# A hybrid transformer layer on one core: the low parts of the gate and branch weights formed on GpSimd

## The chip, the cores and the metric

The kernel runs on one core of one Trainium2 chip. The metric is the device time of one execution in microseconds (us); several runs are timed and their median is given. A separate execution is recorded by the hardware profiler; its trace gives the rows below.

A core has five engines with a queue each: TensorE (PE, matrix products; PEld is its weight load), VectorE (DVE), ScalarE (ACT), GpSimd (POOL) and SyncE (SP, which here issues nearly all DMAs). An engine takes its instructions in the order written into its queue and waits on semaphores for the others.

## What is computed

One layer of a diffusion backbone over 256 latent and 256 context tokens of width 1024, all in fp32:

```
u   = modulate(rmsnorm(x))                       # latent and context tokens
p   = u @ w_in                                   # ten groups of columns
o_h = HGRN2 linear recurrence(p[0..4])           # 8 heads
o_a = grouped-query attention(p[5..7])           # 8 heads, 2 KV heads
y   = sigmoid(p[8]) * (o_h @ w_branch[0]) + sigmoid(p[9]) * (o_a @ w_branch[1])
x   = x + m * rmsnorm(y @ w_out)
x   = x + m * rmsnorm(moe(modulate(rmsnorm(x)))) # top 4 of 32 experts, w_up 1024x2048, w_down 1024x1024
```

p[8] and p[9] are the gates, w_branch[0] and w_branch[1] the two branches; these are what the change touches.

## The kernel before, in words

The first part (the mixer, up to the router) forms its fp32 products from pairs of reduced-precision products. A weight block is split into a high part (`act.copy` to the type fp32r, L240) and a low part, the difference of the block and its high part (`dve.tensor_sub`, L241), and three matmuls replace one (`mm3`, L246): high by high (L248), high weight by low token (L251), low weight by high token (L252). Only L252 needs the low part of the weights.

Weights come in slabs of 1024 rows by 256 columns (1 MB). `slab` (L225) issues one DMA on SP into a raw tile, of which there are three (tag "raw"), and returns a function that splits half a slab (512 rows: a tile of 128 partitions by 1024 numbers) into a tile of the tag "hl", which holds high and low part and of which there are two. So at most two split halves are alive, and the next ScalarE copy waits until TensorE has used up the half before the last. `chan_major` (L254) uses a half in 24 matmuls of 256 columns.

`branch(br, j)` (L695) makes 256 of the 1024 output columns of one branch: a gate slab (tiles wga, hlga; product pga), its sigmoid, a branch slab (wwb, hlwb; product pb), and the product of both on VectorE (L706 for branch 0; L708, L709, and a split of the sum at L711 and L712 for branch 1). The eight `branch` calls make 16 slabs and 32 halves. The four of branch 0 stand between the attention heads (after heads 1, 3, 5 and 7, L714 to L719), the four of branch 1 follow the last head. `attn_head` (L662) has on VectorE the row maximum (L673), the reciprocal (L677) and the scaling of the softmax (L678, tile pr), whose result TensorE transposes (L681, tile ppt). Between the heads VectorE also sums a product of a modulation vector (L192, tile macc).

After the branches come the output projection (slabs wwo), the second norm, the router, and the experts, whose weights (192 pieces of 2 MB, or parts of one) stream through a ring of ten slots (L897). Some ring slots reuse memory of the mixer: the token tiles "u", free once the last gate is done; the tile "oa" (yg), free after the output projection; and three slots of a pool that opens only after the mixer's slabs are released (L835, L837).

The order of the instructions in the queues of the mixer is not the order of the program text: a planner that walks the program with its own costs for each instruction puts them in order, by priority among those that are ready. Matmuls of different products are mixed by it. In the expert part the order of TensorE is kept as written (L846). A change of an engine or a cost can therefore give other orders on all engines of the mixer.

GpSimd has 16 instructions in the kernel before: constants, two masks, and four DMA issues, two of them for the tile bd (L1081).

Of the kernel before, what the change touches and what calls it, by code (L numbers as in the profile page):

```python
# [39 lines left out]
def hybrid_layer(ctx, tc, x, c, ctx_in, c_ctx, w_mod, b_mod, norm_g, w_in, hgrn_lb, hgrn_norm_g,  # L40
# [3 lines left out]
    pe, act, dve, pool = nc.tensor, nc.scalar, nc.vector, nc.gpsimd  # L44
# [46 lines left out]
    def mmps(name):  # L91
        return ps.tile([P, 512], F32, tag="mm", bufs=4, name=name)
# [7 lines left out]
    def raw_tile(name):  # L100
        return ip.tile([P, 2048], F32, tag="raw", bufs=3, name=name)
# [120 lines left out]
        dve.reciprocal(dst, dst)  # L222


    def slab(src, nm, wr=None):  # L225

        wr = raw_tile("w" + nm) if wr is None else wr
        nc.sync.dma_start(wr.rearrange("p (k f) -> p k f", k=KT), src.rearrange("(k p) f -> p k f", p=P))

        def half(hf):  # L230
            hl = ip.tile([P, 2, 4, 256], F32R, tag="hl", bufs=2, name=f"hl{nm}{hf}")
            hi, lo = hl[:, 0], hl[:, 1]
            split(hi, lo, wr[:, hf * 1024:(hf + 1) * 1024].rearrange("p (k f) -> p k f", k=4))
            return hi, lo

        return half

    def split(hi, lo, src):

        act.copy(hi, src)  # L240
        dve.tensor_sub(lo, src, hi)  # L241

    def halves(t):
        return [t[:, 0:4], t[:, 4:8]]
# [9 lines left out]
    def chan_major(sl, mh, ml, n, outs, hfs=(0, 1)):  # L254

        for hf in hfs:
            hi, lo = sl(hf)
            for cc in range(2):
                for kk in range(4):
                    k = hf * 4 + kk  # L260
                    wh, wl = hi[:, kk, cc * P:(cc + 1) * P], lo[:, kk, cc * P:(cc + 1) * P]
                    mm3(outs[cc], (wh, wl), (mh[hf][:, kk, 0:n], ml[hf][:, kk, 0:n]), k,
                        cc == 0 or n == 512, cc == 1 or n == 512)
# [14 lines left out]
    for tt in range(4):  # L278
        src = xt[:, tt] if tt < 2 else xn[:, tt]
# [11 lines left out]
    wi = w_in[0]  # L291
# [18 lines left out]
    def both(sl):  # L310

        hl = [sl(hf) for hf in range(2)]
        return lambda h: hl[h]

    mod_first(0)
    firsts = [(part(slab(wi[:, 2048 + 1024 * d:2304 + 1024 * d], f"f{d}0"), 0),
               [mmps(f"pf0{d}{cc}") for cc in range(2)]) for d in range(2)]
    modulated(0)
    sl_i = slab(wi[:, 1024:1280], "i0", xp.tile([P, 4, D], F32, tag="xn", name="wi0").rearrange("p a b -> p (a b)")[:, 0:2048])
    mod_first(1)  # L320
    for sl, pf in firsts:
# [75 lines left out]
    def hgrn_pair(pr_, qT, gsl, fl3, fc, vt):  # L397
# [101 lines left out]
        for cc in range(2):  # L499
            pc, hs_ = po[:, cc * T:(cc + 1) * T], slice(cc * T, (cc + 1) * T)  # L500
            for tt in range(2):
# [12 lines left out]
        dve.scalar_tensor_tensor(rs, po, hg[:, 0:1], rs, op0=ALU.mult, op1=ALU.mult)  # L514
        dve.tensor_mul(rs, rs, gsl)
        split(ohh[:, 2 * pr_:2 * pr_ + 2].rearrange("p a b -> p (a b)"),
              ohl[:, 2 * pr_:2 * pr_ + 2].rearrange("p a b -> p (a b)"), rs)

# [13 lines left out]
    for pr_ in range(4):  # L532
# [5 lines left out]
        for d in range(2):  # L538
            if pr_ == 0:
                pf = firsts[d][1]  # L540
            else:
                sl = slab(wi[:, 2048 + d * 1024 + c0:2048 + d * 1024 + c0 + 256], f"f{d}{pr_}")
                pf = [mmps(f"pf{pr_}{d}{cc}") for cc in range(2)]
                chan_major(sl, uh, ul, 512, pf)
            for cc in range(2):
                h = 2 * pr_ + cc
                sg = hp_.tile([P, 512], F32, tag="sg", bufs=2, name=f"sg{h}{d}")
                act.activation(sg, pf[cc], AF.Sigmoid)
                a, b = omlb[:, d, h:h + 1], lb[:, d, h:h + 1]
                hs_ = slice(cc * T, (cc + 1) * T)  # L550
                dve.tensor_scalar(fl3[:, d, hs_], sg[:, 0:T], a, b, op0=ALU.mult, op1=ALU.add)
                dve.tensor_scalar(fc[:, d, hs_], sg[:, T:512], a, b, op0=ALU.mult, op1=ALU.add)
# [5 lines left out]
        else:  # L558
            sl = slab(wi[:, 1024 + c0:1024 + c0 + 256], f"i{pr_}")
# [5 lines left out]
        sl = slab(wi[:, c0:c0 + 256], f"q{pr_}")  # L565
# [6 lines left out]
        sl = slab(wi[:, 4096 + c0:4096 + c0 + 256], f"g{pr_}")  # L572
# [32 lines left out]
    sl = slab(wi[:, 6144:6400], "ka")  # L605
    pk = [mmps(f"pk{i}") for i in range(2)]
    tok_major(sl, uh, ul, range(4), [pk[i // 2][:, (i % 2) * 256:(i % 2) * 256 + 256] for i in range(4)])
    for tt in range(4):
        src = pk[tt // 2][:, (tt % 2) * 256:(tt % 2) * 256 + 256].rearrange("p (n d) -> p n d", n=2)
        for g in range(2):  # L610
            act.activation(junk, src[:, g], AF.Square, accum_out=kss[:, tt, g:g + 1])
        rstd_of(kss[:, tt], kss[:, tt], P)
        kr = ac.tile([P, 2, P], F32, tag="kr", bufs=2, name=f"kr{tt}")
        if tt < 2:
            tmp = ac.tile([P, 2, P], F32, tag="rtmp", bufs=1, name=f"ktmp{tt}")
            rope(kr, src, rcs[1], tt, tmp)
        else:
            dve.tensor_tensor(kr, src, view(qkg, [[0, 2], [1, P]], P), op=ALU.mult)
        for g in range(2):
            dve.tensor_scalar(kr[:, g], kr[:, g], kss[:, tt, g:g + 1], None, op0=ALU.mult)  # L620
        pt = trps(f"pkt{tt}")
        for g in range(2):
            pe.transpose(pt[:, g * P:(g + 1) * P], kr[:, g], ident)
        split(khT[:, :, tt * P:(tt + 1) * P], klT[:, :, tt * P:(tt + 1) * P],
              pt[:, 0:256].rearrange("p (g s) -> p g s", g=2))

    sl = slab(wi[:, 6400:6656], "va")
# [8 lines left out]
    for j in range(4):  # L636
        sl = slab(wi[:, 5120 + j * 256:5120 + (j + 1) * 256], f"qa{j}")
        pq = mmps(f"pqa{j}")
        tok_major(sl, uh, ul, range(2), [pq[:, 0:256], pq[:, 256:512]])
        for tt in range(2):  # L640
            src = pq[:, tt * 256:(tt + 1) * 256].rearrange("p (n d) -> p n d", n=2)
# [51 lines left out]
    yh = lp.tile([P, KT, T], F32, tag="yh", name="yh")  # L693

    def branch(br, j):  # L695
        sl = slab(wi[:, 6656 + br * 1024 + j * 256:6656 + br * 1024 + (j + 1) * 256], f"ga{br}{j}")
        pg = mmps(f"pga{br}{j}")
        chan_major(sl, uh, ul, T, [pg[:, 0:T], pg[:, T:512]])
        sg = lp.tile([P, 512], F32, tag="lt", bufs=2, name=f"sgm{br}{j}")
        act.activation(sg, pg, AF.Sigmoid)  # L700
        sl = slab(w_branch[0, br, :, j * 256:(j + 1) * 256], f"wb{br}{j}")
        pb = mmps(f"pb{br}{j}")
        chan_major(sl, *((halves(ohh), halves(ohl)) if br == 0 else (halves(oah), halves(oal))), T, [pb[:, 0:T], pb[:, T:512]])
        yv = yh[:, 2 * j:2 * j + 2].rearrange("p a b -> p (a b)")
        if br == 0:
            dve.tensor_mul(yv, pb, sg)  # L706
        else:
            dve.tensor_mul(sg, pb, sg)  # L708
            dve.tensor_add(yv, yv, sg)  # L709
            hv = yT_hi[:, 2 * j:2 * j + 2].rearrange("p a b -> p (a b)")  # L710
            act.copy(hv, yv)  # L711
            dve.tensor_sub(yT_lo[:, 2 * j:2 * j + 2].rearrange("p a b -> p (a b)"), yv, hv)  # L712

    for h in range(8):  # L714
        attn_head(h)
        for _ in range((0, 0, 1, 1, 1, 1, 2, 2)[h]):
            next(mod2)
        if h % 2 == 1:
            branch(0, h // 2)  # L719
# [3 lines left out]
    for j in range(4):  # L723
        branch(1, j)
# [43 lines left out]
    for j in range(4):  # L768
        sl = slab(w_out[0, :, j * 256:(j + 1) * 256], f"wo{j}")
# [4 lines left out]
        else:  # L774
            pys = [mmps(f"py{j}{tt}")[:, 0:256] for tt in range(2)]
            sl = both(sl)
# [177 lines left out]
    wu, wb = (mp, "wu", 3), (wp, "wb", 3)  # L954
# [311 lines left out]
```

## Time and profile before

| what | value |
|---|---|
| median of 3 runs | 1439.45 us (1437.65 to 1439.98) |
| profiled execution | 1442.47 us |
| its span, first to last instruction | 1440.8 us |
| mean granted TensorE clock | 0.992 of full |
| TensorE busy | 1335.4 us (93%) |
| VectorE busy | 504.6 us (35%) |
| ScalarE busy | 354.5 us (25%) |
| GpSimd busy | 3.8 us (0%) |
| read from HBM | 479.15 MB, 333 GB/s over the span |

The shares are means over the span and hide the stages. The slabs of gates and branches are used from 324 to about 465 us, the output projection runs to 500 us, and the experts fill the rest. A busy TensorE is not one at its peak, since the ends of matmuls are modelled.

### The profile page before, as it was taken

To read this page: it belongs to the slowest core of one execution; us is meant where nothing else is said; L and a number is where in the kernel's file an instruction comes from. 1 tells how busy PE (TensorE), PEld (TensorE's weight loads), DVE (VectorE), ACT (ScalarE), POOL (GpSimd) and SP (SyncE) were. 2 spreads that over 40 slices of the span, in tenths; PEclk is the share of its full clock that TensorE was granted. 3 is DMA by queue.
4 is the path that set the end of the run, shared out by engine and by line. 5 is a ranking of instruction groups with operands and counts; after the bars stand their busy time and mean duration, and the time that the engine had idled before them with its cause. 6 is when DMAs were issued, how large, how long until landed. Compare 5 with 4: busy or idle time off the path is not lost. (4 is left out here: it accounts for less than half of the span.)

```text
span 1440.8 us, 18975 instructions
## 1 busy us (share of the span) xinstructions
PE 1335.4 (93%) x8151; PEld 737.7 (51%) x8151; DVE 504.6 (35%) x917; ACT 354.5 (25%) x648; POOL 3.8 (0%) x16
## 2 busy tenths in 40 slices
PE   5999999999999999999998897999799889889897
PEld 3789798998889943433432342342243233224232
DVE  4598787779865431111101111120011011111012
ACT  5444444457554420100100010010010010001002
POOL 0000000000000000000000000000000000000000
PEclk9999999999999999999999999999999999999999
DMA  9534442237649599999999999999999999999995
GB/s 343 176 118 154 139 148 88 91 118 237 231 150 335 191 403 428 427 426 428 426 428 428 427 427 426 427 428 427 428 427 428 426 428 426 428 427 428 428 428 190
DMA packets 88530, 481.54 MB, mean 334 GB/s; under 512 B 5604, under 2 KB 56264, under 8 KB 62072
## 3 DMA queue, kind: packets, MB, share of 16 engines
q1 hardware_dynamic: 87536, 479.24, 82.1%
q8 instruction: 67, 1.10, 0.3%
q10 hardware_dynamic: 776, 0.84, 0.2%
q14 instruction: 23, 0.19, 0.0%
q0 software_dynamic: 128, 0.16, 0.0%
HBM read 479.15 MB, written 1.08 MB: 333 GB/s over the span
## 5 line engine op out<-in xcount | busy, mean ns | idle before, releaser
L847 PE MATMUL pu<-w,xe 128*64 128x512 f32 x2048 | 459.5, 599 | 58.0 <-DMA w<-in_w_up_dram 57.9
L847 PEld LDWEIGHTS pu<-w,xe 128*64 128x64 f32 x2048 | 143.1, 138 | 357.1 <-issue 251.3
L991 DVE TENSOR_SCALAR gl<-pu 128x512 f32<-128x512 f32 (+1 forms) x33 | 22.2, 675 | 613.3 <-PE pu L847 598.1
L847 PE MATMUL py<-w,aT 128*64 128x512 f32 (+1 forms) x1040 | 227.3, 589 | 2.4 <-ACT aT L1035 1.9
L847 PEld LDWEIGHTS py<-w,aT 128*64 128x64 f32 x1040 | 71.2, 137 | 153.7 <-issue 118.5
L992 ACT ACTIVATE sg<-gl 128x512 f32<-128x512 f32 (+1 forms) x33 | 20.3, 617 | 519.3 <-PE pat L850 481.8
L1050 ACT COPY ysb<-py 128x512 f32<-128x512 f32 x31 | 18.1, 585 | 237.3 <-PE py L847 237.3
L847 PE MATMUL acc<-ysb,cw 64*128 64x512 f32 (+2 forms) x260 | 65.9, 609 | 2.1 <-ACT ysb L1050 1.4
L847 PE MATMUL pgx<-oh,xt 128*128 128x256 f32 x256 | 60.3, 395 | 0.0
L847 PEld LDWEIGHTS pgx<-oh,xt 128*128 128x128 f32 x256 | 46.8, 199 | 16.8 <-issue 5.7
L248 PE MATMUL pf<-uh,hlf 128*128 128x512 f32 x128 | 52.4, 415 | 3.1 <-ACT hlf L240 3.1
L252 PE MATMUL pf<-uh,hlf 128*128 128x512 f32 x128 | 52.9, 415 | 0.0
L251 PE MATMUL pf<-ul,hlf 128*128 128x512 f32 x128 | 52.4, 411 | 0.0
L975 DVE TENSOR_SCALAR xe<-pgx,aff,mod 128x256 f32<-128x256 f32 x32 | 17.4, 544 | 88.9 <-PE pgx L847 88.9
L983 DVE TENSOR_SCALAR ow<-iota,posb,comb 128x128 f32<-128x128 f32 x64 | 19.2, 343 | 57.2 <-PE pcw L850 29.5
L248 PE MATMUL pga<-uh,hlga 128*128 128x256 f32 x128 | 36.9, 288 | 1.6 <-ACT hlga L240 1.6
L252 PE MATMUL pga<-uh,hlga 128*128 128x256 f32 x128 | 36.3, 284 | 1.0 <-DVE hlga L241 1.0
L847 PEld LDWEIGHTS acc<-ysb,cw 64*128 64x128 f32 (+1 forms) x260 | 23.3, 186 | 25.9 <-issue 21.0
L248 PE MATMUL pv<-hli,uh 128*128 128x256 f32 x128 | 36.5, 285 | 0.0
L251 PE MATMUL pv<-hli,uh 128*128 128x256 f32 x128 | 36.3, 284 | 0.0
L251 PE MATMUL pga<-ul,hlga 128*128 128x256 f32 x128 | 36.3, 283 | 0.0
L252 PE MATMUL pv<-hli,ul 128*128 128x256 f32 x128 | 36.2, 283 | 0.0
(388 smaller groups left out, 2053.9 us busy)
## 6 DMA issues: line engine op xcount, KB each, us to landing
w<-in_w_up_dram SPq DMA_DIRECT2D x128, 2048.0 KB, 39.1
w<-in_w_down_dram SPq DMA_DIRECT2D x62, 2048.0 KB, 39.1
wm<-in_w_mod_dram SPq DMA_DIRECT2D x16, 1024.0 KB, 4.9
wm<-in_w_mod_dram SPq DMA_DIRECT2D x16, 512.0 KB, 10.1
wf<-in_w_in_dram SPq DMA_DIRECT2D x8, 1024.0 KB, 5.1
wga<-in_w_in_dram SPq DMA_DIRECT2D x8, 1024.0 KB, 5.2
wwb<-in_w_branch_dram SPq DMA_DIRECT2D x8, 1024.0 KB, 6.0
wi<-in_w_in_dram SPq DMA_DIRECT2D x4, 1024.0 KB
```

What stands on the lines that cost most here:

```text
L248: i = pe.matmul(o, a[0], b[0], start=k == 0 and opens, stop=False)
L251: pe.matmul(o, a[0], b[1], start=False, stop=False)
L252: pe.matmul(o, a[1], b[0], start=False, stop=k == KT - 1 and closes)
L847: tc.keep_in_program_order(pe.matmul(*args, **kw))
L975: dve.tensor_scalar(xe[:, k], pg, aff2[:, k:k + 1], mod[:, 0, 24 + k:25 + k], op0=ALU.mult, op1=ALU.add)
L983: dve.tensor_scalar(ow[:, tt], view(iota, [[0, 2], [1, CAP]]), posb[:, tt, e:e + 1], comb[:, tt, e:e + 1], op0=ALU.is_equal, op1=ALU.mult)
L991: dve.tensor_scalar(gl, glu_ps, 7.0, None, op0=ALU.min)
L992: act.activation(sg, gl, AF.Sigmoid, scale=1.702)
L1050: act.copy(ysb, py)
```

## The change

`split` and `slab` get a parameter for the engine of the subtraction, and `branch` passes GpSimd for both of its slabs. The 32 subtractions of L241 with the tiles hlga and hlwb leave VectorE's queue and enter GpSimd's. The copies on ScalarE, the matmuls, the DMAs, the tiles and their numbers stay. All other splits (the recurrence, the queries, keys and values, the attention weights, the output projection) stay on VectorE.

```diff
-    def slab(src, nm, wr=None):
+    def slab(src, nm, wr=None, eng=None):
...
-            split(hi, lo, wr[:, hf * 1024:(hf + 1) * 1024].rearrange("p (k f) -> p k f", k=4))
+            split(hi, lo, wr[:, hf * 1024:(hf + 1) * 1024].rearrange("p (k f) -> p k f", k=4), eng or dve)
...
-    def split(hi, lo, src):
+    def split(hi, lo, src, eng=dve):
         act.copy(hi, src)
-        dve.tensor_sub(lo, src, hi)
+        eng.tensor_sub(lo, src, hi)
...
     def branch(br, j):
-        sl = slab(wi[:, 6656 + br * 1024 + j * 256:6656 + br * 1024 + (j + 1) * 256], f"ga{br}{j}")
+        sl = slab(wi[:, 6656 + br * 1024 + j * 256:6656 + br * 1024 + (j + 1) * 256], f"ga{br}{j}", None, pool)
...
-        sl = slab(w_branch[0, br, :, j * 256:(j + 1) * 256], f"wb{br}{j}")
+        sl = slab(w_branch[0, br, :, j * 256:(j + 1) * 256], f"wb{br}{j}", None, pool)
```

## Rows read from the trace of the kernel before

**Rows 1.** The page: busy time by engine; chain that ended last, by engine.
```profile
PE 1335.4 (93%) x8151; PEld 737.7 (51%) x8151; DVE 504.6 (35%) x917; ACT 354.5 (25%) x648; POOL 3.8 (0%) x16
DMA 30%; PE 8%; DVE 0%; ACT 0%; issue 0%; DVEq 0%; SPq 0%; ACTq 0%
```

**Rows 2.** Windows: length, busy PE, PEld, DVE, ACT, POOL, clock, DMA share, GB/s.
```profile
324.00:400.00 76.00, 70.04 (x531) 65.09 (x530) 67.25 (x111) 47.45 (x81) 0.00 (x0) 1.00 0.66 222
400.00:465.00 65.00, 64.81 (x513) 61.16 (x513) 41.15 (x61) 32.95 (x47) 1.38 (x3) 1.00 0.69 249
465.00:500.00 35.00, 35.00 (x284) 33.40 (x283) 15.45 (x28) 15.49 (x33) 0.00 (x0) 1.00 0.53 204
...
560.00:1400.00 840.00, 773.07 (x3572) 283.59 (x3568) 115.66 (x216) 79.05 (x158) 0.00 (x0) 0.99 1.01 427
```

**Rows 3.** Timeline of SP's DMA issues, ring pieces: start, time with waits, count.
```profile
466.98 33.97 SPq L925 DMA_DIRECT2D w<-in_w_up_dram  x4
501.00 4.47 SPq L932 DMA_DIRECT2D w<-in_w_down_dram  x2
```

**Rows 4.** Waits of PE, 324 to 400 us: total, times, longest.
```profile
PE ppt L681 <- DVE pr L678: 2.5, 3, 1.2
PE pga L248 <- ACT hlga L240: 1.6, 2, 1.4
PE pga L252 <- DVE hlga L241: 1.0, 1, 1.0
```

**Rows 5.** Line L241, one of the two groups that move: duration min/median/max ns, first and last start.
```profile
L241 DVE TENSOR_TENSOR hlga<-wga,hlga x16: 1215/1224/1227, 325.8 to 453.2; 128x1024 fp32r<-128x1024 f32 x16
```

**Rows 6.** Timeline: one turn of an "hl" tile in branch 1.
```profile
446.62 1.04 ACT L240 CAST hlwb<-wwb 128x1024 fp32r<-128x1024 f32 x1
...
447.69 1.22 DVE L241 TENSOR_TENSOR hlwb<-wwb,hlwb 128x1024 fp32r<-128x1024 f32 x1 [2.10 <-ACT hlwb L240]
...
449.00 0.36 PE L252 MATMUL pb<-oab,hlwb 128*128 128x256 f32 x1
...
451.88 1.05 ACT L240 CAST hlga<-wga 128x1024 fp32r<-128x1024 f32 x1 [1.85 <-PE pb L252]
```

**Rows 7.** Timeline of PE: first high and first low product of one half.
```profile
340.17 0.39 PE L248 MATMUL pga<-uh,hlga 128*128 128x256 f32 x1 [1.44 <-ACT hlga L240]
...
343.75 0.28 PE L252 MATMUL pga<-uh,hlga 128*128 128x256 f32 x1
```

**Rows 8.** Timeline: subtractions that came late, and the matmul behind two of them.
```profile
357.49 1.22 DVE L241 TENSOR_TENSOR hlwb<-wwb,hlwb 128x1024 fp32r<-128x1024 f32 x1 [0.25 <-ACT hlwb L240]
358.80 0.35 PE L252 MATMUL pb<-ohb,hlwb 128*128 128x256 f32 x1
364.97 1.05 ACT L240 CAST hlga<-wga 128x1024 fp32r<-128x1024 f32 x1 [0.65 <-PE pb L252]
367.47 1.22 DVE L241 TENSOR_TENSOR hlga<-wga,hlga 128x1024 fp32r<-128x1024 f32 x1
429.01 1.05 ACT L240 CAST hlga<-wga 128x1024 fp32r<-128x1024 f32 x1 [2.49 <-PE pb L252]
430.35 1.22 DVE L241 TENSOR_TENSOR hlga<-wga,hlga 128x1024 fp32r<-128x1024 f32 x1
431.62 0.39 PE L252 MATMUL pga<-uh,hlga 128*128 128x256 f32 x1
```

**Rows 9.** Groups on DVE, 320 to 425 us: count, busy us, mean ns, idle before.
```profile
L192 DVE SCALAR_TENSOR_TENSOR macc<-wm,csT,macc 128x2048 f32<-128x2048 f32 x7 | 16.4, 2345 | 0.7 <-DMA wm<-in_w_mod_dram 0.7
L678 DVE TENSOR_SCALAR pr<-pr,mx 128x512 f32<-128x512 f32 x16 | 7.8, 486 | 0.5
```

**Rows 10.** Groups on POOL, whole span.
```profile
L759 POOL TENSOR_SCALAR_AFFINE_SELECT tri<-tri 128x128 bf16<-128x128 bf16 x1 | 0.3, 304 | 0.0
L756 POOL MEMSET onesb<- 128x128 bf16 x1 | 0.2, 204 | 243.6 <-DVE ke L416 243.6
L1253 POOL MEMSET const-float32-0.0<- 128x1 f32 x1 | 0.1, 98 | 0.4 <-issue 0.4
```

## The prediction

> **What bounds the kernel now.** I read the page's busy times first, then windows by stage, then the DMA queue of SP, then who waits for whom in the stages that the change touches.
>
> The page says that TensorE is busy for 93% of the span, and the chain that ended last is made of DMA and TensorE only [rows 1]. The windows tell which of the two it is. From 560 us on, the DMA engines are full at 427 GB/s while TensorE is busy 92% of the time: the expert weights set the pace [rows 2]. Before 500 us it is TensorE: 65 of 65 us busy from 400 to 465, 35 of 35 from 465 to 500, with DMA shares of 0.69 and 0.53 [rows 2]. In the queue of SP, the four ring pieces issued from 466.98 on take 34 us to get out, because they wait for memory that the mixer still holds; at 501 us the queue is free and runs full from there [rows 3]. So the end of the kernel is the moment at which the mixer lets go, plus a stream of fixed length. What the mixer gains or loses before 500 us, the end gains or loses, one to one.
>
> In the mixer the change touches two stretches. From 324 to about 425 us the four calls of branch 0 lie between the attention heads; up to 400 us TensorE is idle for 76.00 - 70.04 = 6.0 us, and VectorE is busy for 67.25 of 76 us, so it is close to full too [rows 2]. From about 425 to 465 us the four calls of branch 1 run alone; TensorE is idle for 0.2 us and VectorE has slack [rows 2]. The first stretch has at most 6.0 us to give; the second has nothing to give and can only lose.
>
> **Price of a subtraction on GpSimd.** Before, each of the 32 (16 with the tile hlga, 16 alike with hlwb) takes 1.224 us on VectorE [rows 5]. GpSimd has no instruction of two inputs in this trace. Its nearest rows are a memset of one column (98 ns), one of 128 columns (204 ns) and a select of 128 columns that reads one input (304 ns) [rows 10]. Scaled to 1024 columns, the memset's slope of (204 - 98)/127 = 0.83 ns per column gives 0.95 us, the select's slope of (304 - 98)/127 = 1.62 gives 1.76 us, and twice that slope, if the second input is read after the first, gives 98 + 2 x 1659 = 3.4 us. The range is 0.95 to 3.4 us; I take 2.1 us, a little over the nearest row, because one more input can't be free.
>
> The Trainium skill has a price: "GPSIMD Engine Reference", section 3.1, gives an elementwise add of 2048 fp32 numbers per partition 4497 ns on GpSimd and 2293 ns on VectorE, two inputs sharing one read port. No run here shows it yet; halved, it is an estimate of 2.25 us, by which the sum below would come out about 0.6 us longer, in the same case.
>
> **First stretch, 324 to 425 us.** Gains. (a) One low part came late because VectorE was busy: its copy ended at 364.97 + 1.05 = 366.02 but the subtraction began at 367.47 [rows 8], and TensorE waited 1.0 us for it [rows 4]. On GpSimd it would end at 366.05 + 2.1 = 368.15, where it ended at 368.69: -0.5 us. (b) TensorE waits 2.5 us in three places for the scaled softmax, L678 [rows 4]. VectorE loses subtractions of 1.22 us each from its queue ahead of these, so each wait may shrink by up to its whole; I take 1.5 of the 2.5. The wait of 1.6 us for ScalarE's copy [rows 4] stays, for that copy waits for a free tile. Sum -2.0 us. Loss: a half whose low part was just in time comes 2.1 - 1.22 = 0.88 us later. The one at 357.49 ended 0.09 us before its matmul at 358.80 [rows 8]: +0.8 us. The other halves of this stretch I count as having that much in hand, as the one at 340.17, whose first low product ran 3.6 us after its first high one [rows 7]. Net -1.2 us.
>
> **Second stretch, branch 1.** Here the two "hl" tiles turn in a loop. One turn: copy at 446.62, subtraction from 447.69 to 448.91, first low product at 449.00, next copy into the tile at 451.88 [rows 6]. That is 5.26 us, of which 1.22 is the subtraction, so about 4.0 us without it and without the 0.09 us in hand. In the same time TensorE has to work through two halves, this tile's and the other's. One half holds it from 449.00 to 451.88 [rows 6], 2.87 us, so a turn of more than 2 x 2.87 = 5.74 us stalls TensorE. On GpSimd a turn is 4.0 + 2.1 = 6.1 us: 0.36 us over, in about 5 turns 1.8 us, and on entry the half copied at 429.01 brings its low part at 430.09 + 2.1 = 432.2 instead of in time for 431.62 [rows 8]: +0.6. Together +2.4 us, if TensorE's order stays high, low token, low weight for every block. But the planner can put the 16 matmuls that need only the high part first; that it does so where a low part is late is seen at 340.17, where the first high product runs 3.6 us ahead of the first low one [rows 7]. Then a turn is 1.05 + 2.1 + 8 of 24 matmuls (1.0) = 4.2 us and costs nothing. I take the middle, +1.2 us; the ends are 0 and, at 3.4 us a subtraction, 11 halves x (3.5 - 2.87) = +6.9.
>
> **The rest.** ScalarE's copies, the matmuls and the slab DMAs keep their counts. A raw tile is let go by the subtraction, some 0.9 us later; three raw tiles and the queue's free time in this stretch (DMA share 0.69 [rows 2]) hide that. GpSimd's work of before in this stretch, 1.38 us in 3 instructions [rows 2], two of them DMA issues for bd, could stand ahead of a subtraction; they lie between 426 and 428 us, and the next copy ends only at 430.06 [rows 8]: 0. VectorE's queue gets shorter in the second stretch, where nothing waits for it: 0.
>
> Sum: -1.2 + 1.2 = 0, and with the free choice of the planner about half a microsecond either way. The profiled execution took 1442.47 us for a span of 1440.8; the median of the runs is 3.0 us below it. 1442.47 + 0 less 3.0 is 1439.4 us. About 0.2%, 2.9 us, is what a measurement of this kernel can tell from no change.
>
> **Rivals.**
> *VectorE's relief counts in full.* VectorE's load up to 400 us falls by 12 subtractions, 14.7 of 67.25 us, the planner refills TensorE's gaps, and branch 1 runs with high products first. Then 3 to all 6 us of the idle time go: 1439.45 - 4.5 = 1435 us. For it: VectorE is fuller than ScalarE in this stretch [rows 2], and the largest waits are for it [rows 4]. Against: each low part still comes later than before, unless it stood in the queue for 0.9 us.
>
> *The low part comes too late in branch 1 (slower).* The place is the loop of the two tiles, the price is the turn, and it decides from 5.74 - 4.0 = 1.7 us a subtraction on, if the order is not changed. At 2.75 us, midway between my value and the upper end: 5 turns x 1.0 + 1.2 on entry = 6.2, plus 1.4 in the first stretch, less the gains of 2.0: +5.6, so 1445 us. For it: TensorE has no slack there [rows 2], and its matmul at 431.62 began 0.05 us after the low part that it needed [rows 8]. Against: the order can change, as in [rows 7].
>
> *GpSimd and VectorE take turns at the memory (slower).* 20 subtractions of 2.1 us occupy 42 of 101 us; an L678 that has to wait for one waits 0.42 x 1.05 = 0.44 us on average, 16 of them [rows 9] 7.0 us, in the chain of the heads for which TensorE already waits; half of it reaches TensorE: +3.5. The subtractions wait behind the 7 sums of 2.345 us [rows 9], 16.4 of 101 us, 0.19 us each, 3.8 in all, a quarter of it felt: +1.0. Together +4.5, in which the forecast's 0 for the rest is kept: 1444 us. Nothing in the trace of before shows such a wait, since GpSimd never computes beside VectorE there. The Trainium skill, "SBUF — State Buffer", section "SBUF: two separate sides", states a rule of this kind: the two engines share a port pair that is locked for a whole instruction against a VectorE instruction with two SBUF inputs or in a two-port mode. No run here has shown it yet.
>
> That the change does nothing at all is not among them: GpSimd is given plain tiles in SBUF and an operation of one line.
>
> **Chances.** The forecast (gains and losses cancel, 1436.5 to 1442.3) 0.42; relief in full 0.27; too late in branch 1 0.17; taking turns 0.14. Faster by over 0.2%: 0.26 of the second case and 0.02 of the first, 0.28. Slower by over 0.2%: 0.16 and 0.11 of the last two and 0.03 of the first, 0.30. Within: 0.42. The range of 1433.5 to 1446.5 leaves out a gain of all 6 us and the subtraction near 3.4 us, 0.18 together.
>
> **What would show it.** Right: 32 instructions of L241 on GpSimd at 1.8 to 2.4 us; TensorE's idle time from 324 to 400 us smaller than 6.0 us by 1 to 3; in branch 1 stalls of TensorE on L241 of 1 to 2 us in total; first full DMA window within 2 us of 501. Wrong: VectorE instructions (L678, L192) that take longer than 486 and 2345 ns; subtractions over 2.7 us or spread widely; or an order on TensorE that moves work out of the mixer's end altogether.

## The result and the profile after

The changed kernel takes 1459.44 us (median of 3 runs, 1458.41 to 1459.88) against 1439.45 us: slower, ratio 1.012 with a 95% interval of 1.0089 to 1.0151. The profiled execution took 1459.88 us, its span is 1458.3 us, 17.5 us more than before. Several executions of one kernel differ by more than this spread shows: in later series of 20 to 31 runs the kernel before took 1437.0 to 1448.1 us. The forecast was 1439.4 us, the range ended at 1446.5.

The page of the changed kernel, busy times and chain that ended last [rows 1]:

```profile
PE 1337.1 (92%) x8151; PEld 738.9 (51%) x8151; DVE 487.1 (33%) x885; ACT 356.0 (24%) x649; POOL 85.1 (6%) x48
DMA 35%; PE 3%; DVE 0%; ACT 0%; issue 0%; DVEq 0%; SPq 0%; ACTq 0%
```

VectorE lost 32 instructions and 17.5 us; 32 subtractions of 1.22 us should have been 39 us. So its other instructions grew by some 22 us. GpSimd got 81 us. The windows, columns as in [rows 2]:

```profile
324.00:400.00 76.00, 63.53 (x462) 58.23 (x461) 55.88 (x85) 44.46 (x76) 37.59 (x14) 0.98 0.63 209
400.00:465.00 65.00, 57.61 (x449) 53.39 (x448) 24.64 (x43) 30.14 (x45) 36.79 (x20) 1.00 0.57 206
465.00:500.00 35.00, 33.28 (x265) 31.44 (x264) 15.87 (x20) 15.62 (x24) 8.62 (x4) 1.00 0.70 251
...
560.00:1400.00 840.00, 775.17 (x3588) 284.42 (x3584) 117.65 (x220) 79.67 (x159) 0.00 (x0) 0.99 1.01 427
```

TensorE's idle time grew from 6.0 to 12.5 us in the first window and from 0.2 to 7.4 us in the second; the expert stage is as it was. SP's ring pieces [rows 3] come later by just the span's difference, 518.61 - 501.00 = 17.6 us:

```profile
483.99 34.56 SPq L925 DMA_DIRECT2D w<-in_w_up_dram  x4
518.61 4.45 SPq L932 DMA_DIRECT2D w<-in_w_down_dram  x2
```

Up to that moment, at which the ring is free, TensorE's idle time is 177.00 - 170.85 = 6.2 us before and 194.61 - 173.04 = 21.6 us after. These 15.4 us are nearly all of the 17.6:

```profile
324.00:501.00 177.00, 170.85 (x1326) 160.04 (x1324) 124.82 (x199) 95.90 (x160) 1.38 (x3) 1.00 0.64 227
324.00:518.61 194.61, 173.04 (x1317) 160.45 (x1315) 106.16 (x163) 96.72 (x161) 82.99 (x37) 0.99 0.59 206
```

Who TensorE waited for, 324 to 485 us (total, times, longest), the rows that answer to [rows 4]:

```profile
PE pb L252 <- POOL hlwb L241: 8.0, 8, 2.1
PE pga L252 <- POOL hlga L241: 6.6, 5, 2.5
PE ppt L681 <- DVE pr L678: 3.5, 3, 1.4
```

14.6 us of waits on a low part from GpSimd stand where 1.3 us on one from VectorE stood. That is the bulk of the 17.5. Six of these waits, 8.3 us, come before the last head ends (429.5 us), the other seven, 6.2 us, in branch 1.

The subtractions (line L241, duration ns min/median/max [rows 5]), and VectorE's groups from 320 to 435 us [rows 9]:

```profile
L241 POOL TENSOR_TENSOR hlga<-wga,hlga x16: 2352/2400/4059, 324.7 to 467.9; 128x1024 fp32r<-128x1024 f32 x16
L241 POOL TENSOR_TENSOR hlwb<-wwb,hlwb x16: 2367/2389/4495, 333.0 to 475.1; 128x1024 fp32r<-128x1024 f32 x16
```

```profile
L192 DVE SCALAR_TENSOR_TENSOR macc<-wm,csT,macc 128x2048 f32<-128x2048 f32 x7 | 20.2, 2888 | 2.2 <-DMA wm<-in_w_mod_dram 2.2
L678 DVE TENSOR_SCALAR pr<-pr,mx 128x512 f32<-128x512 f32 x16 | 15.5, 976 | 0.4
L673 DVE TENSOR_REDUCE mx<-pss 128x1 f32<-128x512 f32 x16 | 11.0, 687 | 3.5 <-PE pss L671 3.3
L241 DVE TENSOR_TENSOR plo<-ppt,ph 128x512 fp32r<-128x512 f32 x16 | 10.9, 689 | 14.0 <-ACT ph L240 14.0
```

A subtraction costs 2.4 us (the medians), and up to 4.5. The scaling L678 doubled (486 to 976 ns) and the sum L192 went from 2345 to 2888; the row maximum (687 ns before too) and the split of a PSUM tile (685) did not move. What grew works from SBUF to SBUF; what did not reads PSUM or, like the one-column instructions L674 and L677 (208 and 162 ns before, 212 and 159 after), is very small. The timeline shows how, VectorE and GpSimd from 349 to 357 us:

```profile
349.55 2.33 DVE L192 SCALAR_TENSOR_TENSOR macc<-wm,csT,macc 128x2048 f32<-128x2048 f32 x1
350.03 4.06 POOL L241 TENSOR_TENSOR hlga<-wga,hlga 128x1024 fp32r<-128x1024 f32 x1 [3.46 <-ACT hlga L240]
351.80 2.57 DVE L678 TENSOR_SCALAR pr<-pr,mx 128x512 f32<-128x512 f32 x1
354.05 2.55 POOL L241 TENSOR_TENSOR hlwb<-wwb,hlwb 128x1024 fp32r<-128x1024 f32 x1
```

The sum was first, and the subtraction beside it took 1.66 us longer than alone, about what was left of the sum (to 351.88). Then the subtraction had its turn, and the scaling took 2.57 instead of 0.49 us: to 354.37, just after the subtraction's end at 354.09. Neither is slowed in proportion; each waits for the other's end. In a trace such a wait is no idle time, it stands inside the duration of the one that waits. The longest subtraction, too, started just behind a sum (377.91 to 380.26), and TensorE waited until it ended (GpSimd and PE):

```profile
377.98 4.50 POOL L241 TENSOR_TENSOR hlwb<-wwb,hlwb 128x1024 fp32r<-128x1024 f32 x1 [4.94 <-ACT hlwb L240]
...
382.53 0.38 PE L252 MATMUL pb<-ohb,hlwb 128*128 128x256 f32 x1 [2.05 <-POOL hlwb L241]
```

So the two causes are not apart even here: of the 14.6 us of waiting for low parts, some 3.7 (1.66 and 2.05) come from the subtractions of 4.06 and 4.50 us, which were themselves held up by a sum.

For the subtraction of 4.06 us TensorE stood idle from 351.7 to 354.14; its granted clock, by windows of 1 us, fell in that idle time and stayed at the lower level (1.2 GHz) for some work after it:

```profile
353.00:354.00 1.00, 0.00 (x0) 0.00 (x0) 1.00 (x1) 0.00 (x0) 1.00 (x1) 0.79 0.00 0
354.00:355.00 1.00, 0.86 (x4) 0.86 (x5) 0.37 (x1) 0.00 (x0) 1.00 (x2) 0.50 0.00 0
355.00:356.00 1.00, 1.00 (x6) 1.00 (x6) 0.00 (x0) 0.00 (x0) 1.00 (x1) 0.50 0.88 147
356.00:357.00 1.00, 1.00 (x7) 1.00 (x6) 0.00 (x0) 0.11 (x1) 0.60 (x1) 0.51 0.92 369
```

Its products of 256 columns start 0.21 us apart there; at the full clock it is 0.12 us (as at 442.06 and 442.18 below):

```profile
355.16 0.41 PE L248 MATMUL pga<-uh,hlga 128*128 128x256 f32 x1
355.37 0.41 PE L251 MATMUL pga<-ul,hlga 128*128 128x256 f32 x1
```

So a half-speed microsecond of a busy TensorE costs some 0.43 us. From 320 to 560 us the kernel before is at half speed for 3.4 us and the changed one for 6.8. In each, 3.4 us of it come after the ring is free (from 508.8 and 527.7 us), in the stage that DMA bounds; so the mixer has 0 before and 3.4 after, which adds 1.5 us to the 15.4 of idle time: 16.9 of 17.6 us.

Last, branch 1, where one product of a half waits (GpSimd and PE):

```profile
440.58 2.55 POOL L241 TENSOR_TENSOR hlga<-wga,hlga 128x1024 fp32r<-128x1024 f32 x1 [1.81 <-ACT hlga L240]
...
442.06 0.28 PE L248 MATMUL pga<-uh,hlga 128*128 128x256 f32 x1
442.18 0.28 PE L251 MATMUL pga<-ul,hlga 128*128 128x256 f32 x1
...
443.19 0.38 PE L252 MATMUL pga<-uh,hlga 128*128 128x256 f32 x1 [0.73 <-POOL hlga L241]
```

TensorE does one high product, one low-token product, and stands before the first product that needs the low part, with 14 that need only the high part written behind it.

### The profile page after: what moved, and what is told of

Read it like the earlier page. It is cut to its first block, busy times and chain, and to the rows that moved or that the text cites. A ratio compares the mean times of both kernels' runs of the same rounds, so it can differ in the third digit from the quotient of the medians.

```text
span 1458.3 us, 18981 instructions
## 1 busy us (share of the span) xinstructions
PE 1337.1 (92%) x8151; PEld 738.9 (51%) x8151; DVE 487.1 (33%) x885; ACT 356.0 (24%) x649; POOL 85.1 (6%) x48
## 5 line engine op out<-in xcount | busy, mean ns | idle before, releaser
L241 POOL TENSOR_TENSOR hlga<-wga,hlga 128x1024 fp32r<-128x1024 f32 x16 | 40.6, 2538 | 354.6 <-DVE qr L602 322.9
L241 POOL TENSOR_TENSOR hlwb<-wwb,hlwb 128x1024 fp32r<-128x1024 f32 x16 | 40.9, 2557 | 35.9 <-ACT hlwb L240 35.8
L192 DVE SCALAR_TENSOR_TENSOR macc<-wm,csT,macc 128x2048 f32<-128x2048 f32 x14 | 36.6, 2616 | 10.5 <-DMA wm<-in_w_mod_dram 10.5
L248 PE MATMUL pv<-hli,uh 128*128 128x256 f32 x128 | 36.5, 285 | 0.0
```

What stands on the lines that cost most here:

```text
L192: dve.scalar_tensor_tensor(acc, wr, csT[:, k, 0:1], acc, op0=ALU.mult, op1=ALU.add)
L241: eng.tensor_sub(lo, src, hi)
L248: i = pe.matmul(o, a[0], b[0], start=k == 0 and opens, stop=False)
```

## The experiments

Two theories stood against each other: low parts come too late for the written order of the products ("late"), and GpSimd and VectorE hold each other up ("turns"). All ratios are against the kernel before on the same chip. "Ring free" is the start of SP's first issue of in_w_down_dram (501.00 us before, 518.61 in the changed kernel), less that of before. The stream behind it takes 937.0 to 939.8 us in the traces, and 939.8 in that of before; so a single span is good to some 3 us, and what the mixer lost is read from the ring. The half-speed time is that from 320 to 560 us; the 3.4 us that come behind the ring in the kernel before, the changed one, "only branch 1", "spare", "high first, branch 1" and "four tiles, VectorE" are no part of the mixer.

| kernel | median us | ratio (95%) | span minus before's | ring free minus before's | half-speed us |
|---|---|---|---|---|---|
| changed kernel | 1459.44 | 1.012 (1.0089 to 1.0151) | +17.5 | +17.6 | 6.8 |
| only branch 0 on GpSimd | 1451.72 | 1.0081 (1.006 to 1.0101) | +7.4 | +9.7 | 6.8 |
| only branch 1 on GpSimd | 1448.33 | 1.0052 (1.0032 to 1.0072) | +4.9 | +6.3 | 6.8 |
| high first, all on GpSimd | 1453.34 | 1.0078 (1.0047 to 1.011) | +10.9 | +11.2 | 17.1 |
| spare subtraction on GpSimd | 1477.89 | 1.0255 (1.0214 to 1.0295) | +33.3 | +35.5 | 13.7 |
| high first, branch 1 on GpSimd | 1443.45 | 1.0008 (0.9987 to 1.0028) | +0.5 | +1.9 | 6.8 |
| high first, GpSimd in 4 pieces | 1456.31 | 1.0102 (1.0072 to 1.0131) | +13.9 | +16.1 | 20.5 |
| high first, GpSimd, scaling on ScalarE | 1446.04 | 1.0027 (1.0014 to 1.004) | +5.0 | +7.7 | 10.2 |
| high first, VectorE, scaling on ScalarE | 1444.03 | 1.0023 (1.0011 to 1.0035) | +3.7 | +5.7 | 13.6 |
| twice on VectorE, branch 1 | 1453.08 | 1.0077 (1.0054 to 1.01) | +7.4 | +9.6 | 0 |
| high first, VectorE | 1445.83 | 1.0018 (0.9999 to 1.0038) | +3.7 | +6.5 | 13.7 |
| four tiles, GpSimd | 1450.69 | 1.0065 (1.0047 to 1.0083) | +7.3 | +10.0 | 3.4 |
| four tiles, VectorE | 1449.05 | 1.0041 (1.0022 to 1.006) | +2.0 | +4.8 | 6.8 |

**One branch at a time.** Both calls of `slab` in `branch` pass `pool if br == 0 else dve`, or `br == 1`.

> Only the 16 halves of branch 0 are formed on GpSimd, those of branch 1 on VectorE. If the loss is made in both stretches by low parts that come 1.2 us later than before (2.40 against 1.22 us), this keeps the loss of the first stretch, some 11 to 13 us of the 17.6 by which the trace of the changed kernel moves the ring pieces, and branch 1 runs as before: about 1451 us. If the two engines holding each other up is what costs, the same stretch holds nearly all of it, since VectorE has most of its work there: 1453 to 1456 us.

> Only the 16 halves of branch 1 are formed on GpSimd. Late low parts: the loop of two tiles, cast 1.05, subtraction 2.40, 24 matmuls 2.87 and some 0.1 us of hand-overs, is 6.4 us a turn against 5.74, with stalls of TensorE on L252 of 5 to 6 us in branch 1: about 1445 us. Engines holding each other up: VectorE has little to do there, so 1440 to 1442 us.

TensorE's waits with branch 0 alone, then with branch 1 alone:

```profile
PE ppt L681 <- DVE pr L678: 5.3, 4, 3.0
PE pga L252 <- POOL hlga L241: 4.3, 2, 2.5
PE pb L252 <- POOL hlwb L241: 1.8, 3, 0.8
```

```profile
PE ppt L681 <- DVE pr L678: 2.9, 4, 1.2
PE pb L252 <- POOL hlwb L241: 2.7, 4, 1.0
PE pga L252 <- POOL hlga L241: 1.8, 3, 0.7
```

Neither theory does alone: beside the heads the wait for the scaling doubled (2.6 in the whole stretch before), and branch 1 pays 4.5 us for late parts though VectorE has slack there. By time, the first fits the theory of late parts (1451 us), the second lies above both. The two halves nearly add up to the whole: the ring is later by 9.7 and 6.3 us, 16.0 of 17.6, and the ratios by 0.81% and 0.52%, 1.33 against 1.2%. The two spans add up to 12.3 of 17.5 us, but the 3.7 us between that and the ring lie behind the mixer.

**High products first.** `high_first` stands in for `chan_major` in `branch`:

```diff
+for w, low in ((hi, False), (lo, True)):
+    for cc in range(2):
+        for kk in range(4):
+            if low:
+                pe.matmul(outs[cc], wt, mh[hf][:, kk, 0:T], ...)
+            else:
+                pe.matmul(outs[cc], wt, mh[hf][:, kk, 0:T], ...)
+                pe.matmul(outs[cc], wt, ml[hf][:, kk, 0:T], ...)
```

> All 32 halves on GpSimd as in the change, but the 16 matmuls of a half that need only the high part are written ahead of the 8 that need the low part. Late low parts: TensorE has 1.9 us of work before it needs the low part, the subtraction is 2.4 us, the waits of TensorE on L241 of GpSimd (15.6 us in the changed kernel) fall under 4 us and the time is 1440 to 1445 us. Engines holding each other up: waits move to the head's chain (L678 at 976 ns, L192 at 2888 ns) and the time stays above 1450 us.

> High products first for both branches, and only branch 1 on GpSimd. Two causes theory (late low parts in the written order; the two engines holding each other up while the heads run): the first is taken away by the order and the second by the place, so nothing is left of the loss: 1438 to 1442 us, no wait of TensorE on L241 of GpSimd over 0.5 us in total. A single cause, late low parts: also near 1440. If something else in having the subtraction on GpSimd costs, as its issue or its memory traffic, the 4 to 6 us of branch 1 stay: 1444 to 1447.

> All low parts on VectorE, high products first: the control for the same order with GpSimd (1453 us). Of that kernel's 10.9 us of span, 6 are there by the end of branch 1 and 5 come in the output projection, where its granted clock is 0.5 from 478 to 488 us. If the order of the output projection makes that half-speed stretch and GpSimd only the 6, this kernel takes 1440 to 1445 us, with the half-speed stretch in it. If GpSimd's use brings both, 1437 to 1441 us.

(The 15.6 us of the first expectation, and the 9.3 and 6.3 of a later one, count one wait of 1.1 us twice; the sum is 14.6.) With the order turned, TensorE waits for no subtraction on GpSimd any more. What is left, with all on GpSimd, is the wait for the scaling (here L695):

```profile
PE ppt L698 <- DVE pr L695: 9.4, 7, 2.6
```

```profile
L695 DVE TENSOR_SCALAR pr<-pr,mx 128x512 f32<-128x512 f32 x16 | 15.0, 941 | 0.4
```

With branch 1 alone, where the heads are nearly over, nothing measurable is left of the loss (0.9987 to 1.0028). On VectorE the same order comes out 0.18% longer, at the edge of the noise (0.9999 to 1.0038), and its wait for the scaling is 5.2 us: the order moves the heads' matmuls too. So the 0.78% of the first of the three is probably not GpSimd's alone. Part of it is a half-speed stretch in the output projection, which the first and the last of the three show, and the second, with the same order in both branches, does not; with GpSimd throughout:

```profile
478.00:489.00 11.00, 11.00 (x57) 11.00 (x57) 1.61 (x3) 2.01 (x3) 0.00 (x0) 0.53 0.38 158
```

TensorE is never idle there. The router's small products (32 columns) stand in this stretch, but they stand in the output projection of the kernel before (470.7 to 475.1 us) and of the second kernel (469.5 to 476.5 us) too, at the full clock; they alone do not make it, and what does is open. Less 0.43 of their half-speed time, 7.4 and 5.9 us, the ring is later by 3.8 us with GpSimd and 0.6 with VectorE: an estimate of 3.2 us for GpSimd's company. TensorE's idle time up to the ring says nearly the same, 11.1 against 8.4 us.

**A spare subtraction.** VectorE keeps all its work; GpSimd repeats each of the 32 into a tile that nobody reads.

```diff
+split(hi, lo, src_)                                  # ScalarE and VectorE, as before
+spare = at.tile([P, 4, 256], F32R, tag="spare", ...)
+pool.tensor_sub(spare, src_, hi)
```

> VectorE forms the low parts of all halves as before; GpSimd forms each of the 32 a second time into a spare tile that no other instruction reads, so nothing waits for GpSimd and only its use of the memory beside VectorE is added. Late low parts: no change, 1438 to 1442 us. Engines holding each other up: VectorE's instructions grow (L678 toward 976 ns, L192 toward 2900, the subtractions of L241 over 1.3 us) and part of the loss is there, 1446 to 1456 us.

VectorE's groups in it, 320 to 470 us (L245 is the subtraction, L682 the scaling):

```profile
L245 DVE TENSOR_TENSOR hlga<-wga,hlga 128x1024 fp32r<-128x1024 f32 x14 | 30.8, 2199 | 2.9 <-ACT hlga L244 2.9
L245 DVE TENSOR_TENSOR hlwb<-wwb,hlwb 128x1024 fp32r<-128x1024 f32 x12 | 23.8, 1980 | 1.8 <-ACT hlwb L244 1.7
L682 DVE TENSOR_SCALAR pr<-pr,mx 128x512 f32<-128x512 f32 x16 | 10.5, 654 | 0.5
```

No result of GpSimd is used, yet VectorE's own subtraction goes from 1.22 to 2.1 us and the kernel loses more than in the change. TensorE's longest waits up to the ring (320 to 540 us) are all for VectorE:

```profile
PE pga L256 <- DVE hlga L245: 10.2, 6, 3.0
PE ppt L685 <- DVE pr L682: 9.4, 8, 2.1
PE pb L256 <- DVE hlwb L245: 6.7, 5, 3.4
```

Turns are a cost by themselves. It is not true that nothing waits for GpSimd here: a raw tile is free only when the spare subtraction has read it, and SP's slab loads waited 6.7 us in three places for that (320 to 500 us). How much of the loss comes by this way was not tested; TensorE's waits show it for VectorE's instructions. That the loss is over what was expected fits with both subtractions becoming ready at the same moment, the end of the copy, 32 times; that was not tested apart either. The Trainium skill, "SBUF — State Buffer", section "SBUF: two separate sides", has this as an exclusive lock of a port pair, held for a whole instruction, against VectorE instructions with two SBUF inputs or in a two-port mode; the rows agree, with 976 against 486 ns where the operands are in SBUF and 687 against 687 where one is in PSUM.

**Late without GpSimd.** In branch 1 VectorE makes each low part twice, in the same place.

```diff
+split(hi, lo, src_)
+dve.tensor_sub(lo, src_, hi)      # branch 1 only
```

> No subtraction on GpSimd. In branch 1 VectorE forms each low part twice over, one after the other into the same place, so it is ready some 1.15 us later than before, about as late as GpSimd makes it; the order of the products is as written. Late low parts: the same stalls on L252 as with branch 1 on GpSimd, 4 to 6 us, 1445 to 1447 us. If GpSimd itself is needed for the loss of that stretch: 1438 to 1442 us.

The loss is there with no work on GpSimd, and larger than expected (VectorE also has 16 more subtractions to do). TensorE's waits, 324 to 485 us:

```profile
PE pga L251 <- ACT hlga L243: 3.8, 4, 1.7
PE pb L251 <- ACT hlwb L243: 2.4, 3, 0.9
PE pga L255 <- DVE hlga L236: 1.1, 2, 0.8
```

Most of it shows up as a wait for ScalarE's copy (L243), that is for the tile: it is the turn of the two tiles that is too long, and where in the turn TensorE stands is a matter of order.

**More tiles.** Second halves of the slabs get two tiles of their own.

```diff
-hl = ip.tile([P, 2, 4, 256], F32R, tag="hl", bufs=2, ...)
+hl = (at if own else ip).tile([P, 2, 4, 256], F32R, tag="hb" if own else "hl", bufs=2, ...)
```

> All 32 halves on GpSimd in the written order, with two more tiles for the second halves of a slab (four in all), so that a copy and a subtraction can start two halves earlier. Late low parts: in branch 1 the wait for the tile is gone and the subtraction, 2.4 us against 2.87 us of TensorE per half, is ahead of TensorE; the 6.3 us of waits there go, and part of the 9.3 in the first stretch; what is left is the holding up: 1446 to 1452 us. If it stays at 1456 us or more, the two tiles are not what makes the low part late.

> The kernel before with the same four tiles and all low parts on VectorE. TensorE's waits for a copy (1.6 us) and for a low part (1.3 us) before 400 us can go: 1435 to 1440 us, and it would be the fastest. If the tiles were not what it waited for, 1438 to 1442.

With GpSimd and the written order, all waits on L241 of GpSimd over 0.3 us are gone, and 11.0 us of waiting for the scaling take their place (14.9 us busy, 929 ns each): the low parts are in time, the turns stay. With VectorE it was expected to be the fastest and is slower than the kernel before, by 0.41% (1.0022 to 1.006): its wait for the scaling is 6.4 us, for reasons of order that I did not follow. So an edit that only lets the planner choose other orders can move the time by this much, and no run changes the engine of the subtraction with all orders held.

**Where the turns reach TensorE.** The scaling goes to ScalarE, with all low parts on GpSimd and, as control, on VectorE.

```diff
-dve.tensor_scalar(pr, pr, mx[:, 3:4], None, op0=ALU.mult)
+act.activation(pr, pr, AF.Copy, scale=mx[:, 3:4])
```

> All 32 halves on GpSimd, high products first, and the scaling of the softmax (tile pr) on ScalarE instead of VectorE, so that no instruction of the head's chain on VectorE has all its operands in SBUF. If the chain of the heads behind that one instruction is how the holding up reaches TensorE, 4 to 8 of the remaining 13 us go: 1445 to 1449 us, and TensorE waits for it under 4 us where it waited 9.4. If the sums of L192 are what carries it, 1451 to 1454 us.

> The same two edits (high products first, scaling on ScalarE) with all low parts on VectorE: the control for the run before it. VectorE is full in that stretch and loses 7.8 us, ScalarE gains some 10: 1437 to 1441 us by every theory. If this is as slow as the one with GpSimd, the edits and not GpSimd carry its loss.

1.0027 and 1.0023 (the control was expected at 1437 to 1441 us and is slower): with this one instruction off VectorE, GpSimd costs nothing that the runs can tell, where it was 0.78 against 0.18% with the scaling on VectorE, although the sums L192 still take 2902 ns. TensorE waits for the scaling 2.9 us with GpSimd and 3.7 without. So the runs point to the scaling, in the chain of the heads, as the main way by which the turns reach TensorE. It is not the only one. With the scaling on ScalarE a sum held up by a subtraction kept VectorE from its split of the softmax (tile plo), and TensorE stood for it (GpSimd, VectorE and PE):

```profile
367.12 2.40 POOL L241 TENSOR_TENSOR hlga<-wga,hlga 128x1024 fp32r<-128x1024 f32 x1 [2.38 <-ACT hlga L240]
367.18 4.48 DVE L192 SCALAR_TENSOR_TENSOR macc<-wm,csT,macc 128x2048 f32<-128x2048 f32 x1 [0.75 <-DMA wm<-in_w_mod_dram]
...
372.31 0.58 PE L704 MATMUL poa<-plo,vah 128*128 128x256 f32 x1 [2.46 <-DVE plo L241]
```

For this split TensorE waited 3.7 us in all, 0.3 in the control. Its idle time up to the ring is 8.8 against 7.5 us, and the ring, corrected for half-speed time as above, is later by 3.3 us with GpSimd and earlier by 0.2 without: up to 3.5 us may be left.

**Smaller turns.** GpSimd subtracts 4 times 256 columns.

> All 32 halves on GpSimd, high products first, each subtraction cut into 4 of 256 columns (some 0.65 us each). Holding up for a whole instruction: VectorE waits for a quarter as long, so the scaling of the softmax falls from 941 ns toward 550 to 650 and the time from 1453 to 1443 to 1447 us. Sharing of bandwidth instead of whole instructions: the scaling stays near 900 ns and the time at 1452 us or more.

```profile
L699 DVE TENSOR_SCALAR pr<-pr,mx 128x512 f32<-128x512 f32 x16 | 9.7, 613 | 0.4
```

The scaling fell to 613 ns, as whole-instruction turns have it, and TensorE's wait for it from 9.4 to 6.1 us, but the time did not fall. 128 pieces take 101 us of GpSimd instead of 79, and TensorE was at half speed for 20.5 us, among it again a stretch in the output projection. As a test of the turns it speaks by its row; as a remedy it failed.

## Why the prediction was wrong

The forecast put -1.2 us on the first stretch, +1.2 on branch 1 and 0 on the rest. TensorE's idle time says +9.2, +6.2 and 0, and the clock adds 1.5.

**What bounds the kernel: right.** The mixer's loss went to the end one to one (17.6 us in SP's queue, 17.5 in the span); in the other traces it did to within 0.3 to 2.8 us.

**Price of a subtraction: low.** 2.1 us taken, 2.4 measured alone. The Trainium skill's figure ("GPSIMD Engine Reference", section 3.1), halved to an estimate of 2.25, was nearer than the bounds from rows of other operations; the subtractions in the trace, 2.4 us each in the median, are the measurement that counts.

**The step that failed in both stretches is the reading of the row at 340.17: that TensorE does the high products of a half first and so has work while a low part is late.** On it rest "the planner can put the 16 matmuls that need only the high part first" (branch 1) and "the other halves of this stretch I count as having that much in hand" (first stretch).

**Second stretch.** The planner never does put them first: in both traces the 768 products of gates and branches go high, low token, low weight without one exception within a tile of PSUM. Between 340.17 and 343.75 TensorE did one low-token product of this tile and then products of others, as the trace of before shows (order of time):

```profile
340.39 0.28 PE L251 MATMUL pga<-ul,hlga 128*128 128x256 f32 x1
340.51 0.28 PE L252 MATMUL pb<-ohb,hlwb 128*128 128x256 f32 x1
...
343.55 0.37 PE L252 MATMUL pb<-ohb,hlwb 128*128 128x256 f32 x1
```

The planner fills a gap with another product; it does not turn an order within one. Without that step the working held: at 2.4 us a turn is 6.4 us, 0.66 over in 5 turns and 0.9 on entry, 4.2 us; with branch 1 alone TensorE waited 4.5 us for GpSimd; in the changed kernel it was 6.2, in 7 turns. The forecast had taken the middle of this and 0, so here the step is worth only some 1 to 3 us of the miss; the larger part is in the first stretch. Writing the order by hand did what I had left to the planner.

**First stretch: wrong in sign, and the larger miss.** Loss (one half late, +0.8) was mis-sized: six waits on L241 of GpSimd sum to 8.3 us up to the last head in the changed kernel, where the kernel before waited 1.3 for VectorE's. That the other halves had time in hand was counted from one row, the one misread. Gain (b), 1.5 us less waiting for the scaling, did not come; that wait grew, from 2.6 to 3.5 us, and to 5.3 with branch 0 alone. VectorE's queue did get shorter (the rival of full relief even counted 12 subtractions up to 400 us where the trace of before has 16), but what stands in it got longer.

**The rivals: two of them came true together.** Late low parts (+5.6) and turns (+4.5) were priced well apart but as alternatives, with 0.17 and 0.14. They are two effects of one edit: a subtraction that is slow is late, and one that holds VectorE delays the heads. Where both meet, a subtraction held up by a sum makes the low part later still (the 3.7 us above). Their sum, 10 us, is still short of 17.5, since the first had 1.4 us for late parts in the first stretch (8.3 measured) and the second 1.0 for subtractions held up by the sums (3.7 of these 8.3); but the range should have held the sum.

**Open.** What the new orders of the planner cost or save by themselves; why some of the versions have a half-speed stretch in the output projection; and how much of the turns is left with the scaling on ScalarE. None of the versions beats the kernel before.

## What to carry to other kernels

A subtraction moved to an idle engine is judged by when its result is needed, not by how busy the old engine was: here 1.2 us of lateness in a loop of two tiles was paid by the bounding engine, turn by turn. Work given to GpSimd from SBUF lengthened here those of VectorE's larger instructions that have all operands in SBUF (the scaling from 486 to 976 ns); look for one of them in the chain that feeds the bound before moving anything. When a planner orders the queues, check in the trace which orders it really changes (between products, not within one), and write by hand what has to come first.

## What the runs showed of the hardware that was not expected

A wait between GpSimd and VectorE shows as duration, not as idle time: 0.49 us of scaling recorded as 2.57. A stall of TensorE can cost more than itself: in the wait of 2.5 us from 351.7 us its clock fell, and it came back only after 2.8 us of further work at 1.2 GHz; the waits of 2.1 and 1.9 us up to 382.5 and 395.9 us had no such stretch behind them. With all on GpSimd and high products first, the granted clock also fell with TensorE busy in every record, from 478 to 488 us; the page's busy share says nothing of it, and its cause is open.
